# A bidirectional RWKV-7 and attention trunk: the scan of a head pair in 12 slots of a 64-step projection window, instead of 14

## The chip, the cores and the metric

The kernel runs on one core of one Trainium2 chip. The metric is the device time of one execution in microseconds, as a median of runs. Every profile shown is one execution of the program on that core. The engines are named as in the profile: PE (TensorE matmul) and PEld (its weight loads), ACT (ScalarE), DVE (VectorE), POOL (GpSimd), SP (SyncE, which issues the DMAs).

## What is computed

The reference is an encoder trunk of two layers on 256 tokens of width 2048. A layer normalises its input, multiplies it by one large input projection, and feeds two groups of heads: 16 RWKV-7 heads with a scan in each direction, and 16 heads of windowed attention. Both are gated, put side by side, multiplied by an output projection and added to the input.

```
for l in range(DEPTH):                                   # 2 layers
    h = rms_norm(x, norm_g[l])
    proj = einsum('btd,dc->btc', h, w_in[l])
    rw_in, g_rw, q, k_at, v_at, g_at = split(proj)
    r, k, v, xw, xa = split(bidir_token_shift(rw_in, shift_mu[l]))
    y_rw = rwkv7_branch(r, k, v, xw, xa, ...)            # 16 heads of 64, two directions
    y_at = window_attention(rope(q), rope(k_at), v_at, sink[l])
    mix = concatenate([y_rw * silu(g_rw), y_at * silu(g_at)])
    x = x + einsum('btc,cd->btd', mix, w_out[l])
return rms_norm(x, final_g)

# the scan of a head, one direction (S is 64 x 64)
s_kk = S @ kk_t
S = S * w_t - outer(s_kk, a_t * kk_t) + outer(v_t, k_t);   y_t = S @ r_t
```

The kernel computes the scan in chunks of 64 tokens: a Gram product of the chunk's keys and queries, the inverse of a unit triangular 64 x 64 matrix, and then four chunks in sequence with the state carried between them.

## The kernel before

**The projection stream.** A projection tile of 128 columns takes 16 steps. A step is three matmuls of 128 x 128 on 128 x 256 (L292 to L294): high part by high part, and the two cross terms with low parts. The weights come by DMA as tiles of 128 x 1024 for eight steps; ACT casts each half of them to the high part (`hi`, L222) and DVE subtracts for the low part (`lo`, L224). `hi` and `lo` have two buffers each, so a cast for the tile after next waits for the end of an eight-step tile. A layer's input projection has 864 steps, of which 32 come ahead of the loop, then 13 windows of 64 steps follow; the output projection has 256 steps and no scan beside it.

**Windows and slots.** PE's order is written out by hand (`manual_schedule` for PE alone); on ACT, DVE and POOL a planner chooses the order from priorities and readiness. Only instructions issued through `PA` and `PV` (L237) are kept behind the instruction written before them on their engine. `window` (L394) cuts a window's 64 steps into `SLOTS` slots. At the start of a slot every generator that is listed for it is advanced by one part, up to its next `yield`, and then the slot's share of projection steps is written: four or five of them with 14 slots.

**The chains.** The 16 heads are eight pairs. For pair p the projections lie in window p, and then come three chains, listed in `scans` (L1021) with a lag in windows:

- `scan_p` (13 parts, lag 1 and 2) prepares decays, normalised keys and the bonus. Its matmuls: low-rank products `pza` (L671 to L673, part 1), head sums `pk` (L686, part 3) and bonus sums `pbn` (L686, part 12).
- `scan_i` (16 parts, lag 2, the last two at lag 3) builds the inverse. Gram of direction 0 (L786 into `pg`, masked by DVE into `GE`, L792), Gram of direction 1, then ACT's copies to `AB` (L802), transposes into `pt` (L809, L817), which ACT copies out to `BT` (L822) and the first state `SUV` (L827); then six doubling levels. The first level (L889, L891) is one part, the others two each: `pq` (L899, with the turn of L866) copied by ACT (L902, L870), and `pd` (L908), put into `tv` by a predicated copy on DVE (L910). Part 15 is `pf` (L866, L917 to L922), copied by ACT at L924 and L870; part 16 is `pn` (L931, L935), copied at L937.
- `scan_b` (17 parts, lag 3 and 4, at priority 95) runs the four chunks: `pcc` products (L957, L970, L973, L980), state copies by ACT (L975) and DVE (L982), output products into the bank `py` (L964, L987). Then squares (L998, four pairs of instructions on ACT), a power on POOL (L1000), a product on DVE, transposes of the result (L1007) and the gate.

**PSUM.** The pool `ps_w` (tag `w`) has two buffers of two banks. `pza`, `pk`, `pbn`, `pg`, `pt`, `pq`, `pd`, `pf`, `pn` and the attention's products all take theirs from it, so a third one waits until one of the two before it has been read. `ps_c` has one bank for `y` and one for `c`.

**Which windows.** Scan slots are full in windows 2 to 9 of a layer; windows 10 to 12 hold the end of the last pairs and the attention (`ATT`). In layer 0 some DVE work that sets up the rotary tables is spread over the windows (`ROT`).

Of the kernel before, what the change touches and what calls it, by code (L numbers as in the profile page):

```python
# [9 lines left out]
F32 = mybir.dt.float32  # L10
# [5 lines left out]
AF = mybir.ActivationFunctionType  # L16
# [24 lines left out]

SLOTS = 14

STAGE_P = (([6], [4, 5, 6, 7, 8, 9, 10, 11, 12, 13]), ([2], [2]))
STAGE_P0 = (([], [12, 13]), ([3], [3, 5, 6, 8, 10, 11, 12, 13]))
STAGE_I = (list(range(SLOTS)), [0, 1])
STAGE_B = (list(range(1, 14)), [1, 2, 3, 4])
ATT = [  # L50
    [4, 11],
    [1, 3, 6, 8, 11, 13],
    [0, 2, 5, 7, 8, 10, 12, 13],
]

ROT = {0: [2, 3], 1: [], 7: [3, 6, 9], 8: [1, 4], 9: []}
# [78 lines left out]
def hybrid_trunk_kernel(ctx, tc, xT, wi, wv, wo, par, fing, dup, iup, sink, pos, cst, out):  # L135
# [14 lines left out]
    ps_c = pool("ps_c", 1, space=PSUM)  # L150
# [18 lines left out]
    half = (slice(0, 64), slice(64, 128))  # L169
# [69 lines left out]
    PA, PV = InTurn(A), InTurn(V)  # L239
# [78 lines left out]
    AB, AL, QF = (cp.tile([128, 2, NC, 64], F16, name=n) for n in ("AB", "AL", "QF"))  # L318
# [74 lines left out]

    def window(n, *gens, groups=SLOTS):  # L394

        done = 0
        for i in range(groups):
            for g, at in gens:
                for _ in range(at.count(i)):
                    if g.__name__ == "scan_b":  # L400
                        with tc.high_priority(offset=PRIO_B):
                            next(g, None)
                    else:
                        next(g, None)
            upto = n * (i + 1) // groups
            S.run(upto - done)
            done = upto
# [247 lines left out]
    def layer(l):  # L655
# [120 lines left out]
        def scan_i(p, t):  # L776
            VV, BK, MV = t["v"], t["BK"], t["MV"]
            flat = lambda x: x.rearrange("p d c j -> p (d c) j")
            GE = st("ge", [2, 2, NC, 2, 64], bufs=2)
            GE = [GE[:, h] for h in range(2)]  # L780
            GEd = lambda d: pick(GE[0], every, d * NC * 128, [2 * NC * 128, 2], [128, NC], [1, 128])
            for d in range(2):
                pg = wpair("pg")
                for c in range(NC):
                    for h in range(2):
                        PE.matmul(  # L786
                            pg[:, h, c * 128 : (c + 1) * 128],
                            BK[half[h], d, c, 1 - h : 3 - h, :].rearrange("p s j -> p (s j)"),
                            MV[half[h], d, c].rearrange("p s j -> p (s j)"),
                            start=True, stop=True,  # L790
                        )
                V.tensor_tensor(  # L792
                    GEd(d),
                    pg.rearrange("p h (c x) -> p h c x", c=NC),
                    gm[d].unsqueeze(1).unsqueeze(1).to_broadcast([128, 2, NC, 128]),
                    op=ALU.mult,
                )
                if d == 0:
                    yield
            yield  # L800
            for h in range(2):
                PA.activation(flat(AB[half[h]]), GE[h][half[h]].rearrange("p d c s j -> p (d c) s j")[:, :, 0, :], AF.Copy)  # L802

            pt2 = wpair("pt")
            pts = [pt2[:, h] for h in range(2)]
# [49 lines left out]
            for x in (TC, TT):  # L855
                V.tensor_copy(flat(x), EYE.unsqueeze(1).to_broadcast([128, 2 * NC, 64]))
            t.update(GE=GE, BT=BT)
            yield
            dch = [(d, c, h) for c in range(NC) for d in range(2) for h in range(2)]
            hq = lambda x, d, c, h: x[half[h], d, c, :]  # L860
            hx = lambda x, d, c, h: x[half[h ^ d], d, c, :]
# [79 lines left out]
        def scan_b(p, t):  # L941
            GE, MV, BT, SUV, PC, bv = (t[n] for n in ("GE", "MV", "BT", "SUV", "PC", "bv"))


            pyt = ps_c.tile([128, 512], F32, tag="y", name="py")
            py = pyt[:, 0:256].rearrange("p (c j) -> p c j", j=64)
            for i in range(NC):
                ci = [order[d][i] for d in range(2)]

# [24 lines left out]
                for h in range(2):  # L974
                    A.activation(here(h), pc[half[h], 1], AF.Copy)  # L975
                yield
                if i < NC - 1:
                    for d in range(2):
                        for h in range(2):
                            PE.matmul(pS[half[h], d, :], BT[:, h, d, i, :], SUV[:, d, ci[d], h, :], start=(i == 0), stop=True, skip_group_check=True)  # L980
                    for h in range(2):
                        V.tensor_tensor(  # L982
                            here(h, i + 1), pS[half[h]], pick(PC, half[h], i, [2 * NC - 1 - 2 * i, 2], [0, 64]), op=ALU.mult
                        )
# [36 lines left out]
        def scans(w):  # L1021

            gens = []
            prep = [(w, STAGE_P0[w])] if w < 2 else [(2, STAGE_P[1]), (1, STAGE_P[0])]
            stages = [(lag, scan_p, at[0]) for lag, at in prep]
            stages += [(4, scan_b, STAGE_B[1]), (3, scan_i, STAGE_I[1]), (3, scan_b, STAGE_B[0])]
            stages += [(2, scan_i, STAGE_I[0])]
            stages += [(lag, scan_p, at[1]) for lag, at in prep]
            for lag, scan, at in stages:
                p = w - lag  # L1030
                if 0 <= p < NP:
                    if (scan, p) not in chains:
                        chains[scan, p] = scan(p, L.ts[p])
                    gens.append((chains[scan, p], at))
            return gens
# [71 lines left out]
                    yield  # L1107

        for w in range(NP + 2):
            window(64, *scans(w), *([(setup_, ROT.get(w, [3, 6, 12, 12]))] if l == 0 else []))  # L1110
        att = attend()
        window(64, *scans(NP + 2), (att, ATT[0]))
        window(64, *scans(NP + 3), (att, ATT[1]))
# [32 lines left out]
    setup_ = setup()  # L1146
# [99 lines left out]
```

## Time and profile before

| | us |
|---|---|
| median of three runs | 1186.72 |
| lowest and highest run | 1185.43, 1187.16 |
| span of the profiled execution | 1186.6 |
| PE counted busy | 1160.9 (98%) |
| DVE counted busy | 908.2 (77%) |
| ACT counted busy | 777.3 (66%) |

The span runs from the first to the last instruction of the profiled execution. Matmuls are pipelined and their ends are modelled, so PE's busy time also covers part of its waiting; the starts of its instructions are measured. In the timeline a row gives the start, the time until the end of the last of the merged instructions, the engine, the line and the tiles, and in brackets an idle time of the engine with what ended it.

### The profile page before, as it was taken

The numbers are of one execution on the slowest core, as the hardware profiler recorded it, in microseconds if no ns is written. First come the engines' busy times: TensorE is split into PE (matmuls) and PEld (weight loads), VectorE is DVE, ScalarE is ACT, GpSimd is POOL, SyncE is SP. The second block draws the span as 40 slices with busy tenths as digits, with TensorE's granted clock in tenths as the row PEclk, the third lists the DMA queues.
The fourth block names the chain that finished last, engine by engine and source line by source line (L and its number), as shares of the span: only waits on it lengthen the run. The fifth ranks groups of instructions, "written<-read, shape, count | busy, mean of one in ns | idle before, by whom it ended". The sixth has DMA issues, their size and how long they took to land.

```text
span 1186.6 us, 38095 instructions
## 1 busy us (share of the span) xinstructions
PE 1160.9 (98%) x16151; PEld 1082.7 (91%) x16151; DVE 908.2 (77%) x2017; ACT 777.3 (66%) x1955; POOL 18.7 (2%) x23
## 2 busy tenths in 40 slices
PE   8999999999999999999999999999999999999996
PEld 6988998999889989899999999999999998889996
DVE  6889878987877678766677988887887866786654
ACT  6666776777776666645555766876777666665553
POOL 0000000000000000000000000000000000000000
PEclk9999999999999999999999999999999999999998
DMA  7553333333323434477664443333323334345653
GB/s 257 164 170 123 109 107 116 108 98 115 109 94 122 136 117 142 134 234 236 210 184 165 134 131 114 95 113 117 122 83 109 122 124 132 114 145 190 213 185 123
DMA packets 60410, 166.63 MB, mean 140 GB/s; under 512 B 7728, under 2 KB 22736, under 8 KB 60240
## 3 DMA queue, kind: packets, MB, share of 16 engines
q1 hardware_dynamic: 60240, 164.21, 43.0%
q8 instruction: 126, 2.06, 0.7%
q14 instruction: 44, 0.36, 0.1%
HBM read 157.37 MB, written 4.19 MB: 136 GB/s over the span
## 4 chain that ended last, share of the span: by engine, by line
PE 74%; issue 15%; DVE 7%; ACT 2%; POOL 1%; DMA 1%; SPq 0%; DVEq 0%; POOLq 0%; ACTq 0%
PE pm L292 19%; PE pm L294 16%; PE pm L293 16%; PE pg L786 3%; DVE lo L224 2%; PE pcc L957 2%; PE py L987 2%; PE py L964 1%; PE pcc L980 1%; PE pq L899 1%; PE pcc L970 1%; PE pd L908 1%; PE pza L671 1%; POOL yv L1000 1%; PE pscr L1050 1%
## 5 line engine op out<-in xcount | busy, mean ns | idle before, releaser
L292 PE MATMUL pm<-XH,hi 128*128 128x256 f32 x1664 | 494.2, 297 | 3.9 <-ACT XH L184 1.6
L294 PE MATMUL pm<-XH,lo 128*128 128x256 f32 x1664 | 467.8, 281 | 5.9 <-DVE lo L224 5.8
L293 PE MATMUL pm<-XL,hi 128*128 128x256 f32 x1664 | 467.6, 281 | 0.8 <-DVE XL L185 0.6
L222 ACT ACTIVATE hi<-raw 128x512 fp32r<-128x512 f32 x560 | 328.2, 625 | 190.6 <-PE pm L293 91.8
L224 DVE TENSOR_TENSOR lo<-raw,hi 128x512 fp32r<-128x512 f32 x560 | 369.1, 686 | 102.5 <-ACT hi L222 95.2
L292 PEld LDWEIGHTS pm<-XH,hi 128*128 128x128 f32 x1664 | 313.4, 188 | 19.3 <-ACT XH L184 2.6
L294 PEld LDWEIGHTS pm<-XH,lo 128*128 128x128 f32 x1664 | 313.9, 189 | 8.3 <-DVE lo L224 8.3
L293 PEld LDWEIGHTS pm<-XL,hi 128*128 128x128 f32 x1664 | 314.1, 189 | 1.7 <-DVE XL L185 1.7
L292 PE MATMUL pm<-MH,hi 128*128 128x256 f32 x512 | 144.0, 281 | 0.0
L294 PE MATMUL pm<-MH,lo 128*128 128x256 f32 x512 | 143.8, 281 | 0.0
L293 PE MATMUL pm<-ML,hi 128*128 128x256 f32 x512 | 143.8, 281 | 0.0
L292 PEld LDWEIGHTS pm<-MH,hi 128*128 128x128 f32 x512 | 96.6, 189 | 0.8 <-issue 0.8
L293 PEld LDWEIGHTS pm<-ML,hi 128*128 128x128 f32 x512 | 96.6, 189 | 0.0
L294 PEld LDWEIGHTS pm<-MH,lo 128*128 128x128 f32 x512 | 96.6, 189 | 0.0
L910 DVE CAST_PREDICATED tv<-LV,pd 128x256 f16<-128x256 uint8 x80 | 34.2, 428 | 12.0 <-PE pd L908 11.4
L1065 ACT ACTIVATE mv<-mv,mx 128x257 f32<-128x257 f32 x64 | 31.9, 503 | 17.2 <-DVE mx L1062 17.2
L792 DVE TENSOR_TENSOR ge<-pg,C 128x1024 f32<-128x1024 f32 x32 | 38.8, 1219 | 2.3 <-PE pg L786 2.3
L975 ACT ACTIVATE suv<-pcc 64x128 f32<-64x128 f32 x128 | 34.3, 268 | 9.2 <-PE pcc L973 7.4
L959 ACT ACTIVATE rh<-pcc 128x128 f32<-128x128 f32 x64 | 17.5, 274 | 34.0 <-PE pcc L957 33.6
L902 ACT ACTIVATE QF<-pq 128x256 f16<-128x256 f32 x80 | 30.8, 384 | 12.5 <-PE pq L866 11.7
L786 PE MATMUL pg<-mv,bk 64*128 64x128 f32 x512 | 37.2, 285 | 0.3 <-DVE ge L792 0.3
L786 PEld LDWEIGHTS pg<-mv,bk 64*128 64x128 f32 x512 | 31.1, 187 | 2.4 <-DVE ge L792 0.4
(248 smaller groups left out, 1856.5 us busy)
## 6 DMA issues: line engine op xcount, KB each, us to landing
raw<-wi SPq DMA_DIRECT2D x207, 512.0 KB, 3.7
raw<-wo SPq DMA_DIRECT2D x64, 512.0 KB, 4.2
raw<-wv SPq DMA_DIRECT2D x8, 512.0 KB, 3.6
rrot<-u SPq DMA_DIRECT2D x80, 32.0 KB, 1.9
vg<-xT SPq DMA_DIRECT2D x16, 128.0 KB, 4.1
xd<-vg SPq DMA_DIRECT2D x16, 128.0 KB, 3.5
vg<-xd SPq DMA_DIRECT2D x16, 128.0 KB, 3.6
g<-dup SPq DMA_DIRECT2D x16, 97.0 KB
```

What stands on the lines that cost most here:

```text
L222: A.activation(hi[:, q], raw[:, q], AF.Copy)
L224: V.tensor_tensor(lo[:, q], raw[:, q], hi[:, q].bitcast(F32), op=ALU.subtract)
L292: PE.matmul(pm, wh, rh[:, kk, :], start=(kk == 0), stop=False)
L293: PE.matmul(pm, wh, rl[:, kk, :], start=False, stop=False)
L294: PE.matmul(pm, wl, rh[:, kk, :], start=False, stop=(kk == 15))
L786: PE.matmul(pg[:, h, c * 128 : (c + 1) * 128], BK[half[h], d, c, 1 - h : 3 - h, :].rearrange("p s j -> p (s j)"), MV[half[h], d, c].rearra ...
L792: V.tensor_tensor(GEd(d), pg.rearrange("p h (c x) -> p h c x", c=NC), gm[d].unsqueeze(1).unsqueeze(1).to_broadcast([128, 2, NC, 128]), op= ...
L902: A.activation(t_sub(QF), flat4(pq[:, :, 0:128]), AF.Copy)
L910: V.copy_predicated(t_sub(TC), t_mask, flat4(pd[:, :, 0:128]))
L957: PE.matmul(pc[half[h], 0, d, :], GE[h][r, d, ci[d], 0, :], SUV[r, d, ci[d], h, :], start=True, stop=True)
L975: A.activation(here(h), pc[half[h], 1], AF.Copy)
L1065: A.activation(Sc[:, h, q, 0:257], Sc[:, h, q, 0:257], AF.Exp, scale=0.125, bias=mx[:, q : q + 1], accum_out=den[:, q : q + 1])
```

## The change

`SLOTS` goes from 14 to 12, and the slot lists of all chains are rewritten for it. `scan_i` loses two parts: both directions' Gram products are in its first part, each followed by its own `AB` copies (four copies of 64 x 256 instead of two of 64 x 512), and the first doubling level is in the same part as the transposes. Slot 0 of a window therefore holds `pf` of one pair and both Gram products of the next; slot 1 holds `pn`, the transposes and the first level. `scan_b` of a pair now has 11 parts at lag 3 and six at lag 4: its last output product and squares (part 12) come in slot 0 of the next window, the product on DVE in slot 1, the result's transposes in slot 2. Its output bank `py` is taken in the third part of the first chunk instead of the first. A window's slots now have five or six projection steps.

```
-SLOTS = 14
+SLOTS = 12
-STAGE_P = (([6], [4, 5, 6, 7, 8, 9, 10, 11, 12, 13]), ([2], [2]))
-STAGE_P0 = (([], [12, 13]), ([3], [3, 5, 6, 8, 10, 11, 12, 13]))
+STAGE_P = (([5], [3, 4, 5, 6, 7, 8, 9, 10, 11]), ([2], [0, 2]))
+STAGE_P0 = (([], [10, 11]), ([2], [2, 4, 5, 7, 8, 9, 10, 11]))
 STAGE_I = (list(range(SLOTS)), [0, 1])
-STAGE_B = (list(range(1, 14)), [1, 2, 3, 4])
+STAGE_B = (list(range(1, 12)), [0, 1, 2, 3, 4, 5])
 ATT = [
-    [4, 11],
-    [1, 3, 6, 8, 11, 13],
-    [0, 2, 5, 7, 8, 10, 12, 13],
+    [3, 9],
+    [1, 3, 5, 7, 9, 11],
+    [0, 2, 4, 6, 7, 9, 10, 11],
 ]
...
-                if d == 0:
-                    yield
-            yield
-            for h in range(2):
-                PA.activation(flat(AB[half[h]]), GE[h][half[h]].rearrange("p d c s j -> p (d c) s j")[:, :, 0, :], AF.Copy)
+                for h in range(2):
+                    PA.activation(AB[half[h], d], GE[h][half[h], d, :, 0, :], AF.Copy)
+            yield
...
             t.update(GE=GE, BT=BT)
-            yield
             dch = [(d, c, h) for c in range(NC) for d in range(2) for h in range(2)]
...
-            pyt = ps_c.tile([128, 512], F32, tag="y", name="py")
-            py = pyt[:, 0:256].rearrange("p (c j) -> p c j", j=64)
             for i in range(NC):
...
+                if i == 0:
+                    pyt = ps_c.tile([128, 512], F32, tag="y", name="py")
+                    py = pyt[:, 0:256].rearrange("p (c j) -> p c j", j=64)
                 if i < NC - 1:
...
-            window(64, *scans(w), *([(setup_, ROT.get(w, [3, 6, 12, 12]))] if l == 0 else []))
+            window(64, *scans(w), *([(setup_, ROT.get(w, [3, 6, 10, 10]))] if l == 0 else []))
```

## Rows read from the trace of the kernel before

**Rows 1.** The page: span, and PE's busy time, share and instructions.

```profile
span 1186.6 us, 38095 instructions
...
PE 1160.9 (98%) x16151; PEld 1082.7 (91%) x16151; DVE 908.2 (77%) x2017; ACT 777.3 (66%) x1955; POOL 18.7 (2%) x23
```

**Rows 2.** Two windows: stretch, length, busy PE, PEld, DVE, ACT, POOL, clock, DMA.

```profile
236.40:277.98 41.58, 41.14 (x753) 37.77 (x751) 35.24 (x76) 30.19 (x81) 1.04 (x1) 1.00 0.34 107
...
775.12:816.31 41.19, 41.14 (x752) 37.85 (x750) 34.00 (x72) 29.90 (x81) 1.01 (x1) 1.00 0.35 109
```

**Rows 3.** Timeline of PE: two scan groups in one slot, and each alone.

```profile
878.67 0.28 PE L294 MATMUL pm<-XH,lo 128*128 128x256 f32 x1
878.88 0.45 PE L957 MATMUL pcc<-suv,ge 128*64 128x64 f32 x8
...
879.73 0.28 PE L293 MATMUL pm<-XL,hi 128*128 128x256 f32 x1
...
894.39 0.28 PE L294 MATMUL pm<-XH,lo 128*128 128x256 f32 x1
...
895.06 0.28 PE L293 MATMUL pm<-XL,hi 128*128 128x256 f32 x1
...
1002.80 0.28 PE L294 MATMUL pm<-XH,lo 128*128 128x256 f32 x1
...
1003.61 0.28 PE L293 MATMUL pm<-XL,hi 128*128 128x256 f32 x1
```

**Rows 4.** Timeline of PE: the start of a slot 0, layer 0.

```profile
234.12 0.28 PE L294 MATMUL pm<-XH,lo 128*128 128x256 f32 x1
234.67 0.30 PE L866 MATMUL pf<-EYE,tv 64*64 64x32 f16 x16 [0.27 <-DVE tv L910]
```

**Rows 5.** Timeline of PE and ACT: a slot 12, and below one without delay.

```profile
808.96 0.56 ACT L975 ACTIVATE suv<-pcc 64x128 f32<-64x128 f32 x2
809.31 0.69 PE L987 MATMUL py<-suv,ge 128*64 128x64 f32 x8
809.94 0.30 PE L899 MATMUL pq<-tv,AB 64*64 64x32 f16 x16
...
933.31 0.45 PE L987 MATMUL py<-suv,ge 128*64 128x64 f32 x8
933.70 0.30 PE L899 MATMUL pq<-tv,AB 64*64 64x32 f16 x16
```

**Rows 6.** Timeline of PE and ACT: a slot 0, layer 1.

```profile
814.59 0.30 PE L866 MATMUL pf<-EYE,tv 64*64 64x32 f16 x16
...
815.22 1.16 PE L786 MATMUL pg<-mv,bk 64*128 64x128 f32 x16
816.31 0.39 PE L292 MATMUL pm<-XH,hi 128*128 128x256 f32 x1
...
814.51 1.15 ACT L222 ACTIVATE hi<-raw 128x512 fp32r<-128x512 f32 x2 [1.58 <-issue]
815.57 0.40 ACT L446 ACTIVATE g<-g 128x256 f32<-128x256 f32 x1
815.87 0.57 ACT L924 ACTIVATE q<-pf 128x512 f16<-128x512 f32 x1
816.35 0.37 ACT L870 ACTIVATE tt<-pf 128x256 f16<-128x256 f32 x1
```

**Rows 7.** Timeline of ACT: the first of a pair's squares and what follows the last.

```profile
810.10 0.22 ACT L998 ACTIVATE ysq<-py 128x64 f32<-128x64 f32 x1 [0.59 <-PE py L987]
...
810.91 0.40 ACT L902 ACTIVATE QF<-pq 128x256 f16<-128x256 f32 x1
```

**Rows 8.** The page, costliest groups: busy, mean ns of one, idle before.

```profile
L792 DVE TENSOR_TENSOR ge<-pg,C 128x1024 f32<-128x1024 f32 x32 | 38.8, 1219 | 2.3 <-PE pg L786 2.3
```

**Rows 9.** Timeline of PE: the first steps of window 11, layer 0.

```profile
436.61 0.40 PE L294 MATMUL pm<-XH,lo 128*128 128x256 f32 x1 [1.01 <-DVE lo L224]
```

**Rows 10.** Timeline of ACT: the copies from the transposes, layer 1.

```profile
824.64 0.81 ACT L822 ACTIVATE bt<-pt 128x768 f32<-128x768 f32 x1
825.47 1.55 ACT L827 ACTIVATE suv<-pt 64x256 f32<-64x256 f32 x4
```

## The prediction

> **What bounds the kernel now.** I began with the engine totals of the page [rows 1]: TensorE is counted busy for 1160.9 of 1186.6 us. Ends of matmuls are modelled there, so the figure can't tell work from waiting inside it. I then read the sums over two whole windows [rows 2]: 41.58 us for a window of layer 0 and 41.19 us for one of layer 1, TensorE busy almost throughout, VectorE 34 to 35 us, ScalarE 30 us. The work is the same, so 0.39 us of the first is waiting that the busy time hides. From here on I go by starts of matmuls in the timeline.
>
> Inside the projection a matmul starts every 0.118 us, so a step of three takes 0.354 us, and the 64 steps of a window 22.7 us. The other 18.5 us of [rows 2] are scan matmuls and the way to them and back. TensorE runs in the order written, so two things can move the time: how often it changes between projection and scan, and where a matmul finds its operand or its PSUM pair unready.
>
> **Part 1, fewer round trips.** The timeline has the same two scan groups together and apart [rows 3]. From the last projection matmul before to the second one after it takes 1.06 us with both groups in one slot; alone, L908 takes 0.67 and L957 0.81. Two start intervals of 0.118 belong to the projection each time. Together: 0.82; apart: 0.43 + 0.57 = 1.00, or 1.01 before rounding. A round trip costs 0.19 us. I counted them by going through the slot lists. In windows 2 to 9 all 14 slots have scan matmuls, and afterwards all 12: 16 fewer a layer. Window 10 goes from 13 to 12. Window 11 goes from 6 to 8, because the last output product (L987) and the transposes of the result (L1007) now come in its slots 0 and 2. That is 15 a layer, 30 in all: 30 x 0.19 = **-5.7 us**.
>
> By the Trainium skill (TensorEngine Tiling (Array Packing), section Key Properties) changing the tiling mode drains the array, whichever modes they are. L957 is 128*64 and L908 64*64, so that rule leaves a mode change inside the joined slot and only half of the saving; the sum would be 2.9 us higher. The pair in [rows 3] differs in mode and still saves 0.19, so I keep the whole saving and carry the rule as a rival.
>
> **Part 2, two waits that lose their place.** In slot 0 the last doubling turn (L866 into pf) waits for the predicated copy of slot 13: it starts 0.55 us after the projection matmul before it [rows 4], where 0.21 is usual, so 0.34 is waiting. The nine such starts in windows 4 to 8 and layer 1's window 9 are late by 0.34 to 0.51 in layer 0 and by 0.10 to 0.27 in layer 1, 2.4 us in all. After the change six steps (2.1 us) instead of five and L987 lie between: **-2.4 us**. In slot 12, L987 of the last chunk waits for its second state copy (L975), which ScalarE runs behind a cast: the group needs 0.63 us where the undisturbed one needs 0.39 [rows 5]. Nine groups have this, 0.24 to 0.31 each: 2.4 us. L987 moves behind six steps: **-2.4 us**. Both bounds are zero and these sums.
>
> **Part 3, a new wait in slot 0.** The pool "w" has two PSUM pairs. Slot 0 now wants three: pf, first Gram, second Gram. The third must wait until ScalarE has read pf, by L924 and then L870. From the start of pf the row of the timeline gives [rows 6]: casts until 0.98, L446 until 1.28, L924 until 1.76, L870 until 2.13; the first Gram is issued by 1.72. The change also puts the four squares of the pair two before (L998) into slot 0; they are ready before pf is done, are written ahead of its copies and have a higher priority. They hold ScalarE for 0.81 us [rows 7]. So L870 ends at 2.13 + 0.81 = 2.94. TensorE now begins the slot with L987 (0.39), then pf (0.63) and the first Gram (1.09): 2.11. The second Gram waits 0.83 us. In windows 4 to 8 that is 4.15 us a layer. In window 3 there are neither squares nor L987: 2.13 - 1.72 = 0.41. In window 9 no gate is evacuated just before; I take 0.4. Two layers: 2 x 4.96 = **+9.9 us**. Behind this wait in TensorE's queue stand all projection matmuls; behind the copies on ScalarE stand the casts, which have eight steps of lead. Bounds: 0.35 a window if one cast (half of the pair, 0.53) comes after the copies, and 1.4 if another pair of that size comes in between.
>
> **Part 4, the smaller pieces.** Window 2 has a third product in its slot 0, too: the bonus sums (L686) of pair 0, since the list of that window gains slot 0 and pair 0 is one part ahead of the later pairs. They need a pair that the first Gram's mask product frees: 1.22 us [rows 8] against the second Gram's 1.09, so 0.13 at least and 0.69 more if one low-part subtraction goes before; I take 0.6, near the lower end because nothing else presses there: **+1.2 us** (0.3 to 1.6 in all). At the start of window 11 a projection matmul waits 1.01 us for VectorE's low parts [rows 9], in both layers, where the second scores and the pair's normalisation meet in slots 11 to 13. They come to lie three slots apart: **-2.3 us** with the interval itself (0 to -3). The two ScalarE copies of L802 become four of half the size, about a quarter of a microsecond more a pair on an engine with 11 us free in a window: nothing, as long as that room is in slots 0 and 1. The first doubling level in slot 1 needs these copies. Second Gram at 2.94 + 1.09, mask 1.22, copies about 0.8: 6.1 after the start of slot 0. By my estimate from the same terms (4.03 for slot 0's matmuls, 2.0 for five steps and the trip, 1.5 for the groups ahead) slot 1 reaches that level at about 7.5. Taking the output bank at the third part of a chunk costs nothing: its first product stood in that part already, and slot 2, where the bank's old content is read, lies ahead of slot 3. The tail of the loop, the output projection and the DMAs are the same.
>
> **Sum.** 1186.6 - 5.7 - 2.4 - 2.4 + 9.9 + 1.2 - 2.3 = 1184.9 for the profiled execution, whose span is 0.1 below the median of the runs (1186.7); I leave it at **1184.9 us**. Outside the profile about 0.2% can be told from no change, 2.4 us: below 1184.3 is faster, above 1189.1 slower.
>
> **Rivals.** *Slower: ScalarE runs over in slots 1 and 2.* Slot 1 has three PSUM pairs as well, and the next slot opens a pair that the transposes or the first level hold. The five copies from the transposes take 0.82 + 1.55 us [rows 10]. From the end of the transposes to the second level there are the first level (0.4), five steps with their trip (2.0) and the sums and products at the head of slot 2 (0.9): 3.3 us, against 2.4. It decides from the point where a pair of casts (1.06, [rows 6]) is ahead of these copies: with 3.43 the slack is overdrawn by 0.1, with the copy of L937 (about 0.5) by 0.6. At 0.4 in 16 windows: +6.4, 1191.3 us. For it speaks that in the present trace casts do stand ahead of such copies; against it that the casts are released by the end of an eight-step tile, which falls late in slot 1.
>
> *Faster: the squares come between the casts.* Then the second cast goes behind L870, and the wait is 0.35 instead of 0.83: ten windows give -4.8, 1180.1 us. For it: priority; against it: in [rows 6] the pair starts 0.08 before the slot, so its second cast would start at about 0.45 (half of the pair), when the products of L987 are hardly out.
>
> *Near nothing: round trips save half*, as the rule on mode changes has it: +2.9, 1187.8 us. Against it speaks the one pair of [rows 3].
>
> **How the numbers follow.** Forecast 0.45 (1182.4 to 1187.4 from the bounds of parts 2 and 4), slower rival 0.20, faster rival 0.23, half saving 0.12. Faster by over 0.2%: the faster rival and 0.19 of the forecast, 0.42. Slower: its rival and 0.02 of the tails, 0.22. Within: 0.36. The range reaches from inside the faster rival's spread to about the middle of the slower one's: 1178.5 to 1191.0.
>
> **What would show it.** Right: 254 instead of 284 trips by the slot lists; the start of pf and L987 without delay; in slot 0 an interval of about 0.8 us between the two Grams that ends with L870, in windows 4 to 8 of both layers, and squares before L924 on ScalarE. Wrong: no such interval (faster), or starts that come late at the first or second level in slots 1 and 2 with L937, L822 or L827 as the releaser (slower); trips at unchanged total scan time (half saving). Most uncertain is the order that ScalarE's work takes, which the program's planner chooses.

## The result, and the profile after

The changed kernel takes **1190.9 us** (median of 9 runs, 1189.8 to 1193.4) against 1187.1 for the kernel before (9 runs beside it): a ratio of 1.0034, 95% interval 1.0025 to 1.0044. It is slower by 0.34%, where 1184.9 and a small gain were forecast. The profiled execution went from 1186.6 to 1189.3 us.

The page, its span and engine totals, as in [rows 1]:

```profile
span 1189.3 us, 38176 instructions
...
PE 1152.2 (97%) x16151; PEld 1081.0 (91%) x16151; DVE 910.1 (77%) x2017; ACT 792.6 (67%) x1987; POOL 20.7 (2%) x23
```

TensorE executes the same 16151 matmuls, is counted busy 8.7 us less than before, and the span is longer: it waits more, and the busy time shows this only because the new waits are long enough to be seen as idle. The list of TensorE's waits (what waits, for what; total, times, longest) names them in its first lines:

```profile
PE pg L786 <- ACT tt L867: 15.3, 14, 2.5
PE pbn L686 <- DVE ge L792: 4.1, 2, 2.1
PE pm L294 <- DVE lo L224: 2.9, 6, 1.2
```

The last of these in the kernel before:

```profile
PE pm L294 <- DVE lo L224: 5.8, 11, 1.2
```

The lines of the code have moved by two or three: L867 is the turn copy that was L870, L921 was L924, L863 was L866, L985 was L987, L996 was L998. So the second Gram (L786) waits 14 times, once in each of windows 3 to 9 of both layers, for the second copy out of pf; the bonus sums wait twice, in window 2 of each layer, for the first Gram's mask product; and the waits for low parts are half of those before.

The sums over window 5 of layer 1 (stretch, length, busy time of PE, PEld, DVE, ACT, POOL, clock, DMA share, GB/s), to be set beside the second line of [rows 2]. A stretch runs from the window's first projection step to the next one's, so that slot 0 of the next window lies at its end:

```profile
778.97:820.47 41.50, 40.43 (x753) 37.53 (x751) 34.38 (x71) 31.06 (x82) 1.28 (x1) 1.00 0.34 108
```

41.50 us against 41.19, though two round trips are gone. The slot 0 at its end, in the timelines of PE and ACT, is the counterpart of [rows 6]:

```profile
816.12 0.45 PE L985 MATMUL py<-suv,ge 128*64 128x64 f32 x8
816.50 0.30 PE L863 MATMUL pf<-EYE,tv 64*64 64x32 f16 x16
...
817.14 1.16 PE L786 MATMUL pg<-mv,bk 64*128 64x128 f32 x16
819.38 1.16 PE L786 MATMUL pg<-mv,bk 64*128 64x128 f32 x16 [1.07 <-ACT tt L867]
...
816.16 0.63 ACT L222 ACTIVATE hi<-raw 128x512 fp32r<-128x512 f32 x1 [1.36 <-issue]
816.82 0.22 ACT L996 ACTIVATE ysq<-py 128x64 f32<-128x64 f32 x1
...
817.62 0.43 ACT L446 ACTIVATE g<-g 128x256 f32<-128x256 f32 x1
817.92 0.64 ACT L222 ACTIVATE hi<-raw 128x512 fp32r<-128x512 f32 x1
818.44 0.61 ACT L921 ACTIVATE q<-pf 128x512 f16<-128x512 f32 x1
818.92 0.41 ACT L867 ACTIVATE tt<-pf 128x256 f16<-128x256 f32 x1
```

The mechanism of part 3 is here as it was described: pf is complete at about 817.2, but ScalarE is busy with a cast, the four squares, L446 and the other cast until 818.44, and only then reads pf. The second Gram begins when L867 has ended. From Gram to Gram it takes 2.24 us, of which 1.09 are the first Gram: 1.15 of waiting, where 0.83 was forecast.

### The profile page after: what moved, and what is told of

Same layout as the page of the kernel before. It is cut to its first block, busy times and chain, and to the rows that moved or that the text cites. A ratio compares the mean times of both kernels' runs of the same rounds, so it can differ in the third digit from the quotient of the medians.

```text
span 1189.3 us, 38176 instructions
## 1 busy us (share of the span) xinstructions
PE 1152.2 (97%) x16151; PEld 1081.0 (91%) x16151; DVE 910.1 (77%) x2017; ACT 792.6 (67%) x1987; POOL 20.7 (2%) x23
## 3 DMA queue, kind: packets, MB, share of 16 engines
q8 instruction: 126, 2.06, 0.7%
## 4 chain that ended last, share of the span: by engine, by line
PE 67%; issue 16%; DVE 7%; ACT 7%; DMA 2%; SPq 0%; POOL 0%; DVEq 0%; POOLq 0%; ACTq 0%
PE pm L292 17%; PE pm L293 14%; PE pm L294 14%; DVE lo L224 3%; ACT hi L222 2%; PE pcc L952 2%; PE pcc L978 2%; PE pg L786 1%; PE py L959 1%; DMA raw<-wi 1%; PE pq L896 1%; PE pd L905 1%; ACT ysq L996 1%; PE pcc L965 1%; PE py L985 1%
## 5 line engine op out<-in xcount | busy, mean ns | idle before, releaser
L786 PE MATMUL pg<-mv,bk 64*128 64x128 f32 x512 | 36.6, 284 | 15.3 <-ACT tt L867 15.3
L786 PEld LDWEIGHTS pg<-mv,bk 64*128 64x128 f32 x512 | 30.9, 187 | 18.8 <-ACT tt L867 17.9
L237 ACT ACTIVATE AB<-ge 64x256 f16<-64x256 f32 x64 | 26.6, 416 | 29.3 <-DVE ge L792 28.6
L907 DVE CAST_PREDICATED tv<-LV,pd 128x256 f16<-128x256 uint8 x80 | 34.5, 431 | 4.1 <-PE pd L905 2.8
L434 DVE TENSOR_TENSOR u<-pm,rb 128x256 f32<-128x256 f32 x52 | 21.1, 407 | 16.8 <-PE pm L294 16.7
```

The source lines that it names most:

```text
L237: return lambda *a, **k: tc.keep_in_program_order(getattr(self.engine, name)(*a, **k))
L786: PE.matmul(pg[:, h, c * 128 : (c + 1) * 128], BK[half[h], d, c, 1 - h : 3 - h, :].rearrange("p s j -> p (s j)"), MV[half[h], d, c].rearra ...
L907: V.copy_predicated(t_sub(TC), t_mask, flat4(pd[:, :, 0:128]))
```

## The experiments

All times are medians; "before" beside them is 1187.3 to 1187.9 in every set. In the first texts I count 16 windows with a wait in slot 0; there are 14, since window 2 has no pf. Each edit moves the line numbers by a few, so the tiles' names tell which instruction is meant. The cuts of code show the lines that matter; `...` marks what is left out.

### What a round trip costs

**split** adds trips and nothing else to the kernel after:

```
 for g, at in gens:
+    if i in (4, 6) and g.__name__ == "scan_i" and i in at:
+        S.run(2); ran[0] += 2
...
-S.run(upto - done)
+S.run(upto - done - ran[0]); ran[0] = 0
```

> The kernel after with two more round trips in each of 16 windows and nothing else: in slots 4 and 6 two of the slot's projection steps are written between the slot's products of the chunk recurrence and those of the doubling. 32 trips. Theory (0.19 us a trip, whatever groups meet): +6.1, 1197.0 us. Rival (a pair of joined groups of different tilings pays the drain anyway, so that a trip saves half): +3, 1194 us. If trips were worth nothing: 1191 us.

Measured: 1198.4 us, 7.5 more than after. (Window 2 has only one group in these slots, so it is 28 trips and not 32.) Window 5 of layer 1:

```profile
784.77:826.71 41.94, 40.87 (x753) 37.67 (x751) 34.93 (x71) 31.19 (x82) 1.28 (x1) 1.00 0.33 107
```

41.94 against 41.50: two trips cost 0.44, or 0.22 each. Adding up only the intervals around the scan groups gives 0.38, or 0.19 each, the price read from [rows 3]. At 28 trips that is 5.3 to 6.2 of the 7.5; most of the rest lies in windows 7 and 8 of layer 0, which grew by 1.46 and 0.82 where the steady ones grew by 0.44. They hold the longest wait and the slow stretch that the last section shows. So a trip is worth about what part 1 took, and the rival of half a saving (+3 in place of 7.5) is out.

A change of tiling inside a joined slot is not free all the same. In the kernel before, the first matmul behind L957 starts 0.59 us after the last projection matmul (878.67 and 1002.80 in [rows 3]), whether it is L908 in the joined slot or a projection matmul where L957 is alone:

```profile
879.26 0.30 PE L908 MATMUL pd<-QF,tt 64*64 64x32 f16 x16
...
1003.39 0.39 PE L292 MATMUL pm<-XH,hi 128*128 128x256 f32 x1
```

Apart, two groups make four changes of mode; joined, three. The 0.19 us of [rows 3] is already the difference between the two for groups of 128*64 and 64*64, and those that split drew apart have the same modes, so nothing is left to be halved. The Trainium skill (TensorEngine Tiling (Array Packing), section Key Properties) has every change of tiling mode drain the array; these starts do not speak against that, but half a saving does not follow from it.

### What sets the second Gram's wait

**nosq** leaves the squares out:

```
-for c in range(NC):
-    A.activation(ysq[:, c], py[:, c], AF.Square, accum_out=yv[:, c : c + 1])
-V.tensor_scalar(yv, yv, 1.0 / 64, LNX_EPS, ...)
+V.tensor_scalar(yv, py[:, :, 0], 0.0, 1.0, ...)
```

> The kernel after with the eight squares per pair and their row sums left out (the norm factor is 1, so the output isn't the reference's). It takes 0.81 us from ScalarE ahead of pf's copies in slot 0. Theory (the pair rule, with ScalarE's queue setting its size): the wait of the second Gram falls from 1.15 us to 0.3 to 0.6 in windows 4 to 8, and the longest ones (2.5) go: -7 to -10 us, less what the level in slot 1 then waits for pn's copy, as in the run gap3: 1182 to 1187 us. Rival (the casts, not the squares, set the wait): 1190 us.

Measured: 1181.4 us, 9.5 less than after, slightly more than the 9 at most that I expected. The line of the waits:

```profile
PE pg L786 <- ACT tt L867: 5.5, 14, 1.7
```

From 15.3 to 5.5: the squares' place in ScalarE's queue is two thirds of this wait. What is left stands behind the casts and L446. The edit does one thing more: the scaling on VectorE no longer waits for the squares. So the 9.5 us are not the price of the squares on ScalarE alone; pffp and best1, below, take the two apart.

**pffp** leaves nothing out, but has ScalarE take pf's copies before the squares:

```
-stages += [(4, scan_b, ...), (3, scan_i, ...), ...]
+stages += [(3, scan_i, ...), (4, scan_b, ...), ...]
...
+with tc.high_priority(offset=PRIO_TC):
     A.activation(FN..., pf[:, :, 0:T], AF.Copy)
     turned()
```

> The kernel after with pf's part written first in slot 0 (ahead of the last output products and the squares) and its two copies at the planner's higher priority, so that ScalarE takes them before the squares; nothing is left out. Theory (the squares ahead of the copies make the wait long; leaving them out took 9.5 us): the wait of the second Gram falls from 1.15 us to about 0.4 (casts remain ahead) in windows 4 to 8 and the long ones go; pf meets its own level's copy again, about 0.2 in 16 windows (+3): 1181 to 1186 us. Rival (VF of slot 1 comes late instead, as in the run gap3): 1188 us or above.

Measured: 1186.1 us, ratio 0.9982 (0.9973 to 0.9992) to before, 0.1 above the upper end of what was expected. The waits:

```profile
PE pg L786 <- ACT tt L867: 5.5, 14, 1.7
...
PE pq L886 <- ACT vf L935: 3.1, 11, 0.3
```

The second Gram waits as little as with no squares at all, so it is their order and not their being there. pf's own wait, for which I had allowed 3 us, did not come: each pf starts 0.21 us after the projection matmul before it. The second line is new: the rival had its share, the first level in slot 1 waits 0.28 us for the copy of pn (VF). VectorE's timeline in slot 0 of this kernel says why:

```profile
816.91 0.28 DVE L854 COPY tv<-EYE 128x512 f16<-128x512 f16 x1
817.90 0.17 DVE L998 TENSOR_SCALAR yv<-yv 128x4 f32<-128x4 f32 x1 [0.70 <-ACT ysq L997]
817.98 2.35 DVE L792 TENSOR_TENSOR ge<-pg,C 128x1024 f32<-128x1024 f32 x2
```

A scaling of four numbers a row (L998) waits 0.70 us for the last square, and the first Gram's mask product, whose operand is complete since about 816.8, stands behind it in VectorE's queue. AB's copies wait for the mask, and VF stands behind them on ScalarE. This led to best1, below.

**gap3** leaves the order as it is and gives the copies time, by three projection steps between the two Grams:

```
 # in scan_i, after the first Gram's copies
+if d == 0:
+    S.run(3); ran[0] += 3
```

> The kernel after, with three projection steps of the slot written between the two Gram products of slot 0 (the slot keeps its five or six steps in all, so there is one more round trip in each of 16 windows). Theory (the loss is the second Gram's wait for the PSUM pair that pf holds, 16.3 us over both layers in the trace of after): the three steps take about 1.2 us and cover the wait; 16.3 go, 16 round trips at 0.19 come (3.0), and the bonus sums in window 2 (4.2) lose part of their wait too: 1174 to 1178 us, with no interval between the last step and the second Gram. Rival (fewer and larger slots save nothing, or ScalarE's copies turn up as the wait of a later slot): the wait moves, and the time stays at 1187 or above.

Measured: 1189.0 us. The wait went, as expected; the time did not follow. Waits, and ScalarE's timeline in slot 1:

```profile
PE pq L893 <- ACT vf L941: 9.7, 14, 0.7
...
PE pg L790 <- ACT tt L874: 1.2, 1, 1.2
```

```profile
819.52 0.85 ACT L238 ACTIVATE AB<-ge 64x256 f16<-64x256 f32 x2 [0.62 <-DVE ge L796]
...
820.58 0.59 ACT L941 ACTIVATE vf<-pn 128x512 f32<-128x512 f32 x1
```

Slot 1 has three pairs too: pn, the transposes, the first level. The level takes pn's pair and waits for VF, which is behind AB's copies. In the kernel after, the wait in slot 0 lets ScalarE catch up before slot 1; without it, 9.7 us come back one slot later, and the added trips take most of the rest.

**gaps2** puts three more steps between pn and the transposes (the same two lines ahead of pt):

> As the run gap3, and three projection steps also between pn and the transposes in slot 1. In gap3 the waits of the second Gram went (15.3 to 1.2 us), and the first level in slot 1 began to wait for pn's copy (9.7 us, 14 times 0.69): slot 1 too has three pairs. Theory: with a second pause that wait goes as well, 16 more trips cost 3.0: 1189.0 - 9.7 + 3.0 = 1182.3, 1180 to 1184 us. Rival (the copies are simply too many for ScalarE around slots 0 to 2): the wait goes on to slot 2 or 3, 1187 us or above.

Measured: 1204.8 us, far off. The level's wait for VF is gone. The bonus sums in slot 2, which take the pair of the level, wait for the level's copies instead (8.5 us, 14 times 0.6), and in window 2 the first level waits 3.3 us for the copies from the transposes, in each layer. These make 15.1 of the 22.5 us above my 1182.3; the rest I did not follow up.

**gramfirst** writes the Grams and masks ahead of pf, and AB's copies behind it:

```
-stages += [(4, scan_b, ...), (3, scan_i, ...), ...]
+stages += [(4, scan_b, ...), (2, scan_i, [0]), (3, scan_i, ...), ...]
...
 # in scan_i, behind the Grams and masks
+yield
+for d in range(2):
     for h in range(2):
         PA.activation(AB[half[h], d], ...)
```

> The kernel after, with both Grams and their masks written ahead of pf in slot 0, and the copies to AB behind pf (pf of the pair before reads AB). No round trip is added. Theory: pf then waits for the first Gram's mask product (1.22 us, against 1.09 of the second Gram) and not the Gram for pf's two copies: 0.13 to 0.5 in each of 16 windows in place of 16.3 in all, so 8 to 14 us less, 1177 to 1183 us. Rival (the chain through pf to pn is what counts): pf comes two Grams later (2.2 us), its copies end after slot 1 has begun, and pn waits about 0.7 us or more in each window: 1185 us or above.

Measured: 1193.5 us. Now pf is the third, and waits for VectorE as long as the Gram did for ScalarE:

```profile
PE pf L865 <- DVE ge L792: 19.1, 14, 2.6
```

I had priced this wait at the mask product's length less the second Gram, 0.13 to 0.5. It is 1.36 on the mean. The rival's time came, but not by its way: pn waits 0.4 us in all, as in after. The wait is long because VectorE comes to the mask late, after the casts' low parts, a gate product and the scaling that waits for the squares. It is the mistake of the bonus sums in part 4 once more: an instruction's own length is no measure of when its engine gets to it.

### The bonus sums in window 2

**pbn** moves them out of slot 0:

```
-STAGE_P0 = (..., ([2], [2, 4, 5, 7, 8, 9, 10, 11]))
+STAGE_P0 = (..., ([2], [2, 4, 5, 7, 8, 10, 11]))
```

> The kernel after, with one part fewer of pair 0's preparation in window 1, so that its bonus sums leave slot 0 of window 2. Theory: the two waits of 2.1 us for the first Gram's mask product go, and the second Gram of window 2 has no third product behind it: 1186.7 us (-4.2). Rival (the wait was cover for something late in the same window, such as casts or the preparation of pair 1): 1190 us or above.

Measured: 1190.5 us, ratio 1.0030 (1.0016 to 1.0043): the rival. The two windows that the stall touched, in layer 1, after and then pbn:

```profile
633.10:661.65 28.55, 26.17 (x231) 25.23 (x230) 26.53 (x50) 16.42 (x35) 0.00 (x0) 1.00 0.55 177
661.65:696.54 34.89, 33.96 (x563) 31.28 (x561) 29.25 (x58) 25.34 (x58) 0.00 (x0) 1.00 0.40 127
```

```profile
631.26:657.30 26.04, 25.80 (x228) 24.93 (x226) 23.43 (x45) 15.58 (x33) 0.00 (x0) 1.00 0.53 176
657.30:694.07 36.77, 34.80 (x565) 31.91 (x563) 32.46 (x63) 26.19 (x61) 0.00 (x0) 1.00 0.42 133
```

28.55 + 34.89 = 63.44 became 26.04 + 36.77 = 62.81. Of the 2.1 us wait, 0.6 is gained: the transposes now wait for the second Gram's mask and the level for AB, which the wait had covered.

### Each part alone

In these runs the other lists are adapted to 13 slots, which the cuts leave out.

**gram2** (13 slots, both Grams in slot 0, the level in its own slot):

```
-SLOTS = 12
+SLOTS = 13
...
 t.update(GE=GE, BT=BT)
+yield
```

> The other part alone: 13 slots, both Grams in slot 0, the first doubling level in its own slot 2, and the squares in slot 12, as in the kernel before. Theory: the second Gram still waits for pf's copies (a third pair in slot 0), but the squares (0.81 us) no longer stand in front of them: about 0.6 us in each of 16 windows in place of 1.15, so +9.6, and -2.9 and -2.4 as in the run level2: 1189 to 1193 us. Rival (the order on ScalarE, not the pair, is the cause): without the squares no wait is left, 1180 to 1184 us.

Measured: 1189.9 us, in the theory's range. The second Gram waits 10.7 us in all (14 times), less than the 15.3 with the squares in this slot and more than nothing. It is also more than the 5.5 of nosq, which has no squares there either. Between the starts of the two Grams the steady windows have 0.58 of waiting in gram2 and 0.33 in nosq, and window 9 has 1.48 and 0.30. In nosq L985 (0.39 us) goes ahead of pf, which leaves ScalarE more time; that this is the whole difference is not shown.

**level**, **level2**, **level3** and **level4** (13 slots, the Grams in two slots and AB copied as in the kernel before, the level beside the transposes) differ in the slots of the bonus sums and of the next pair's preparation (the four new lines of STAGE_P in this order):

```
+if d == 0:
+    yield
...
-STAGE_P = (([5], [3, ..., 11]), ([2], [0, 2]))
+STAGE_P = (([5], [3, ..., 12]), ([2], [2]))
+STAGE_P = (([6], [4, ..., 12]), ([3], [1, 3]))
+STAGE_P = (([6], [4, ..., 12]), ([4], [1, 4]))
+STAGE_P = (([6], [4, ..., 12]), ([5], [1, 5]))
```

> One part of the change alone: 13 slots, the Grams in two slots as in the kernel before, the first doubling level beside the transposes, the lists adapted. 269 round trips against 284 (before) and 254 (after). Theory: no second Gram wait; 15 trips at 0.19 save 2.9 us; of the two old waits (pf on the predicated copy, last products on the state copy, 2.4 us each over the program) about half stays, since a slot has five steps against four or five: 1180 to 1184 us. Rival (a round trip saves half or nothing, and the losses of after come from the larger slots): 1186 us or above.

Measured: 1278.8 us, by my lists and not by the part: bonus sums, transposes and level shared slot 2, and the level waited for the last copy of the transposes.

> The first doubling level beside the transposes, alone, with the Grams in two slots (13 slots), and the bonus sums moved to slot 3, so that no slot holds more than the two PSUM pairs that there are. (In the run level the bonus sums shared slot 2 with the transposes and the level, three pairs, and the level waited 3.5 us for the last transposes copy, 16 times.) Theory (what costs is a third pair in a slot; a round trip costs 0.19): no wait of a level or a Gram for a pair; 15 trips fewer, 2.9 us, and about half of the two old waits, 2.4: 1180 to 1183.5 us. Rival (fewer slots don't save): 1186 or above.

Measured: 1189.4 us.

> The run level2 (13 slots, the first level beside the transposes, the Grams in two slots) with the bonus sums in slot 4 instead of 3, where they waited 0.37 us for the pair that the first level held, 14 times. Theory (no wait for a pair is left): 1189.4 - 5.1 = 1184.3, 1182.5 to 1185.5 us. Rival (the wait goes to the next user of the pair): 1188 us or above.

Measured: 1203.8 us.

> The run level2 (13 slots, level beside the transposes, Grams apart) with the bonus sums in slot 5, which holds one pair otherwise (slot 3: two with the level's result still read; slot 4: two with the preparation of the next pair, which made level3 wait 18.1 us). Theory (a third pair in a slot is what costs): no wait for a pair, 1189.4 - 5.1 = 1184.3, 1182.5 to 1185.5 us. Rival: another wait of the kind turns up, 1187.5 us or above.

Measured: 1189.1 us, ratio 1.0007 (0.9997 to 1.0016). The first waits of the first three:

```profile
PE pq L888 <- ACT suv L827: 55.1, 16, 3.5
```

```profile
PE pbn L686 <- DVE tt L894: 5.1, 14, 0.4
```

```profile
PE pza L671 <- DVE tv L909: 18.1, 14, 2.1
```

In level and level3 it is a third user in one slot (the first level in slot 2, the preparation in slot 4); in level2 the bonus sums follow the transposes and the level, and their slot begins before the level's copies are done. In level4 the list is clear of these, and the time is that of before (1.3 us above it, inside the interval). What took the gain is mostly in slot 6, and no pair is short there: the group of head sums (L686), L980, L987 and L907 takes 1.89 us in ten windows, where the same group takes 1.29 in gram2, and 8.0 us more in all with the four other windows. The second half of `ip` (VectorE) and the copy `tt` (ScalarE), operands of its first and last products, come late (window 5 of layer 1):

```profile
794.31 0.78 PE L686 MATMUL pk<-ip,BONES 128*128 128x256 f32 x2
...
795.87 0.30 PE L907 MATMUL pd<-QF,tt 64*64 64x32 f16 x16 [0.16 <-ACT tt L869]
```

So what the level beside the transposes brings alone is not shown by these four runs, as each has a new wait of my lists in it. By an estimate from these figures level4 without its 8.0 us would take 1181 us, but no run has such lists.

### Slot 0 away from the casts

**pf6** and **gram6** begin the windows six projection steps later, for pffp and for gram2:

```
+S.run(6)
 for w in range(NP + 2):
...
-window(64, (att, ATT[2]))
+window(58, (att, ATT[2]))
```

> As the run pffp, and the windows of the scan begin six projection steps later (six steps ahead of window 0, six fewer in the last), so that slot 0 falls six steps after the end of a projection tile and the tile's casts are over when pf's copies come. Theory: nothing is ahead of the copies, the second Gram's wait is 0 to 0.2 us; against after -14 to -16, with 3 for pf's own wait: 1175 to 1181 us. Rival (the casts then delay AB's copies and VF, and the level in slot 1 waits): 1184 us or above.

> The run gram2 (13 slots, both Grams in slot 0, the first level in its own slot, squares in slot 12), with the windows begun six projection steps later. Theory: gram2's second Gram waited 10.7 us for pf's copies behind casts; with the casts gone from slot 0 that falls below 2: 1178 to 1183 us. Rival (the wait was set by something else than the casts): as gram2, 1188 to 1191 us.

Measured: 1255.1 and 1198.1 us. The second Gram's wait is gone from both lists, and others are in its place; the first of pf6, and below that of gram6:

```profile
PE pq L887 <- ACT vf L936: 16.4, 14, 1.3
PE pm L295 <- DVE lo L225: 14.3, 11, 2.4
```

```profile
PE pza L672 <- DVE bv L238: 13.5, 14, 1.4
```

For pf6 it is the rival, and by far more than I gave it. For gram6 it is neither: the wait went with the casts, and the time went up by 8.2 us against gram2. Every due time in the lists is off by six steps, and the casts meet other copies than before; which of these made which wait I did not take apart.

### A version that is faster than both

**best1** is pffp with the scaling off VectorE, **best2** that with the bonus sums moved as in pbn:

```
-V.tensor_scalar(yv, yv, 1.0 / 64, LNX_EPS, ...)
+G.tensor_scalar(yv, yv, 1.0 / 64, LNX_EPS, ...)
```

> The run pffp (pf's part first in slot 0, its copies ahead of the squares) with the scaling of the squares' sums on GpSimd in place of VectorE. In pffp this scale, which waits for the last square, stands in VectorE's queue ahead of the first Gram's mask product, which starts 1.2 us after its Gram; AB's copies, and behind them VF, follow, and the first level in slot 1 waits 0.28 in 11 windows (3.1 us). Theory: the mask starts 0.6 to 0.8 earlier and that wait goes: 1186.1 - 3.1 = 1183.0, 1181.5 to 1184.5 us. Rival (VF comes late for ScalarE's load alone): 1185.5 us or above.

> The run best1 with pair 0's bonus sums out of slot 0 of window 2, as in the run pbn. There the 4.2 us of that wait came back by 3.0 in slots 1 and 2 of the same window (the transposes waited for the second Gram's mask, the level for AB's copies). With the mask earlier, theory: 1.5 to 2.5 us less than best1. Rival (as in pbn): within 1.3 us of best1.

Measured: **1181.6 us**, ratio 0.9948 (0.9934 to 0.9961), and **1180.2 us**, ratio 0.9937 (0.9924 to 0.9949) to before; against after, 10.7 us less. Both beat before. Of best1, VectorE's timeline in slot 0 and window 5 of layer 1:

```profile
813.39 0.29 DVE L854 COPY tv<-EYE 128x512 f16<-128x512 f16 x1
813.59 2.43 DVE L792 TENSOR_TENSOR ge<-pg,C 128x1024 f32<-128x1024 f32 x2
```

```profile
773.99:814.68 40.69, 40.43 (x753) 37.52 (x751) 34.11 (x71) 31.09 (x82) 1.20 (x2) 1.00 0.35 111
```

The mask follows the copy of the identity at once, AB and VF are in time, and the line of the level's wait for VF is gone from the list. A window takes 40.69 against 41.50 of after and 41.19 of before [rows 2]. The two profiled executions of pffp and best1 are 5.2 us apart. Of these, 3.8 lie in windows 3 to 9, where the wait was; 1.5 lie in window 2 of layer 1 (36.42 and 34.92), where TensorE's granted clock fell in pffp's execution and not in best1's (last section). So not all of the step from 1186.1 to 1181.6 need be the scaling. The squares are all there in best1, and it takes what nosq took without them. The second Gram still waits 5.5 us in all. best2 is 1.4 lower, just short of what I expected; the two intervals overlap, so that this step is not shown for certain.

**yvonly** and **before_yv** have that one line alone, on the kernels after and before:

> The kernel after with the scaling of the squares' sums on GpSimd, nothing else. Theory: the second Gram's wait of 15.3 us is set by ScalarE (squares and casts ahead of pf's copies) and stays; the mask has no such wait behind the squares, but nothing waits for AB in this kernel: 1190.9, within 1.5 us. Rival (VectorE's queue is part of the loss): 1188 us or below.

> The kernel before with the scaling on GpSimd. Theory: the squares lie in slot 12 there, no Gram's mask stands behind them, and nothing changes: 1187.4, within 1.5 us. Rival (the gain of the run best1 has nothing to do with the fewer slots): 1184 us or below.

Measured: 1193.7 and 1187.9 us. So the line gains nothing by itself, and best1's gain needs the fewer slots and the copies ahead of the squares. yvonly missed its range by 1.3 on the slow side with the same two waits as after (15.3 and 4.1); the last section has what differs.

## Why the prediction was wrong

- **Part 1 held.** 254 trips by the slot lists, and split confirms 0.19 (0.22 by whole windows).
- **Part 2 held.** Neither wait is left. (The nine starts of pf that were late before are those of windows 4 to 7 in layer 0 and 4 to 8 in layer 1, not the windows that the text names; their sum of 2.4 us is right.) Added over all scan groups of the timeline, with the new waits taken out, the trips and the old waits together gave back 14.4 us, not the 10.5 of parts 1 and 2; about 4 us are small delays in other slots that I had not listed, and did not take apart now.
- **Part 3 failed in its size.** By starts of matmuls the 14 waits sum to 16.3 us, against 9.9. Window by window: 1.15 in place of 0.83 in nine of the ten windows 4 to 8 (9 x 0.32 = 2.9 us), since the first cast begins 0.04 after slot 0 and not 0.08 before it (0.12), 2.28 pass from there to L921 and not 2.17 (1.36 in [rows 6] and 0.81 for the squares), L867 takes 0.41 and not 0.37, and the Gram begins 0.05 after its end; 0.58 in place of 0.41 in window 3; 1.12 in place of 0.4 in window 9, since the copies have the squares ahead of them there as well, and L533 in place of L446; and 2.57 in place of 0.83 in window 8 of layer 0. That one is an activation table load, in ScalarE's timeline there:

```profile
318.17 1.28 ACT L446 ACT_TABLE_LOAD   x1
319.47 0.42 ACT L446 ACTIVATE g<-g 128x256 f32<-128x256 f32 x1
319.79 0.61 ACT L222 ACTIVATE hi<-raw 128x512 fp32r<-128x512 f32 x1
```

  It stood in the trace of before at the same place in ScalarE's order, but there the next to need pf's copies or its pair came a slot later. My upper bound for a window was 1.4, and all but this one are below it. I took the value of the one timeline I had, with the squares put in, as if ScalarE's queue in slot 0 were the same in every window. The condition of the faster rival did come true, the squares between the casts, but not what it drew from it: the second cast still went ahead of pf's copies, and the wait was longer and not 0.35. The step that failed is "The second Gram waits 0.83 us. In windows 4 to 8 that is 4.15 us a layer", with the 0.4 taken for window 9 behind it.
- **Part 4 failed at the bonus sums**: 2.06 us in each layer in place of 0.6. VectorE in window 2 of layer 1, and TensorE's wait:

```profile
658.44 1.28 DVE L224 TENSOR_TENSOR lo<-raw,hi 128x512 fp32r<-128x512 f32 x2
659.63 0.42 DVE L447 SCALAR_TENSOR_TENSOR vg<-g 128x256 f32<-128x256 f32 x1
659.97 2.35 DVE L792 TENSOR_TENSOR ge<-pg,C 128x1024 f32<-128x1024 f32 x2
...
661.34 0.47 PE L686 MATMUL pbn<-th,BONES 128*128 128x256 f32 x2 [2.06 <-DVE ge L792]
```

  I allowed for one low-part subtraction ahead of the mask; there are two and a gate product. The step is "I take 0.6, near the lower end because nothing else presses there".
- **The rest of part 4 held.** The wait at the start of window 11 is gone, and with it some smaller ones: inside the projection 3.4 us are saved in place of 2.3, a slow stretch (below) already deducted. AB's smaller copies and the output bank cost nothing in this kernel.

Put together: forecast -10.5 - 2.3 + 9.9 + 1.2 = -1.7; measured in the profiled execution -14.4 - 3.4 + 16.3 + 4.2 = +2.7. Both sides of the sum were too small, the losses by 9.4 and the gains by 5.0. The place, the releaser and the windows were right; the sign was lost in the sizes of two terms, above all the second Gram's wait (6.4 too small; with 9.9 there the measured terms would give -3.7) and then the bonus sums (3.0). That 1190.9 lies inside the stated range, just below its upper end of 1191.0, is luck: the range was drawn there for the slower rival. That rival, ScalarE running over in slots 1 and 2, gave nearly the time measured but is not what happened: no group there waits in the steady windows of after. It comes to life only when slot 0 stops waiting, as gap3 shows.

## What to carry to other kernels

Before merging slots, count the users of a scarce buffer in each: with two PSUM pairs, most of the new waits seen here (0.3 to 3.5 us each) were those of a third user, or of one that came before the readers were done (in level4 it was an operand that came late), and taking one such wait away moved it to the next unless the engine that frees the buffer was relieved too. Price such a wait by the whole queue of the engine that frees the buffer at that moment (casts, squares, gate, copies), not by the last instruction's length. A tiny instruction that waits (the scaling of four numbers) in front of a large one in an in-order queue is worth moving to an idle engine, but in these runs only where something waited behind it (best1, and not yvonly or before_yv).

## What was not expected of the hardware

After the longest waits, the granted clock of TensorE fell from 1.00 to 0.50, the lower of its two levels (1.2 of 2.4 GHz). Around the 2.5 us wait in layer 0, kernel after (columns as above, the clock is the third number from the end):

```profile
319.00:321.00 2.00, 0.00 (x0) 0.00 (x0) 1.08 (x3) 1.99 (x5) 0.51 (x1) 1.00 0.01 4
321.00:323.00 2.00, 1.79 (x20) 1.67 (x21) 1.86 (x3) 0.82 (x3) 0.00 (x0) 0.89 0.41 102
323.00:325.00 2.00, 2.00 (x11) 2.00 (x11) 1.97 (x5) 1.00 (x3) 0.00 (x0) 0.50 0.41 160
```

Window 8 of layer 0, which begins there, takes 43.13 us against 41.64 in layer 1: 1.5 us that no list of waits shows, as the matmuls are busy and slow. The run pbn has the same wait of 2.5 us there and no fall, and its window 8 takes 41.65. The two, after first:

```profile
322.30:365.43 43.13, 42.09 (x752) 39.03 (x750) 32.24 (x65) 30.35 (x83) 1.01 (x1) 0.96 0.33 103
```

```profile
321.90:363.55 41.65, 40.61 (x752) 37.68 (x750) 32.10 (x65) 30.37 (x83) 1.01 (x1) 1.00 0.33 106
```

After the 2.05 us wait of the bonus sums it fell in yvonly and not in the profiled execution of after (two microseconds behind the wait in layer 1, yvonly first):

```profile
664.00:666.00 2.00, 2.00 (x11) 2.00 (x10) 1.51 (x3) 0.52 (x2) 0.00 (x0) 0.50 0.21 57
```

```profile
662.00:664.00 2.00, 2.00 (x32) 1.80 (x32) 1.97 (x5) 0.91 (x3) 0.00 (x0) 1.00 0.63 206
```

Window 2, which follows, takes 36.45 and 36.40 us in the two layers of yvonly, against 35.14 and 34.89 in after: 2.8 us together, nearly all of the 3.0 between these two profiled executions (1192.3 and 1189.3). It is seen over all executions by their mean granted clock: of the nine of after, the two at 0.990 and 0.991 took 1193.4 and 1192.6 us, the four at 0.994 and 0.995 took 1189.8 to 1190.7. The one execution of yvonly at 0.993 took 1191.0, where the three of after at 0.993 took 1190.9 to 1191.5; its other four lie at 0.988 to 0.992. So at the same clock the two kernels agree, and the 1.3 us by which yvonly missed its range go with the clock; whether its edit makes the clock fall more often, five executions don't show. Whether the clock falls differs between kernels with the same wait, between the layers of one kernel and between its executions; what decides it I did not find. A difference of 1 to 3 us between kernels that have such waits can hold a share of it.
